# A decoder layer with a retrieval of experts: a new flow of gathers, copies moved beside the last heads, and work of the first stages dealt out anew

## The chip, the core and the metric

The kernel runs on one core of a Trainium2 chip. The metric is the device time of one execution in microseconds (us), lower is better. TensorE multiplies matrices into PSUM, VectorE and ScalarE (ACT) work on vectors, GpSimd (POOL) also issues the gathers, SyncE (SP) issues most other transfers.

## The reference

One layer of a hybrid decoder on 512 tokens of width 2048, in 32-bit floats: adaLN (a shift, a scale and a gate per feature from the vector c), a joint projection into differential attention and an mLSTM, an output projection, and a retrieval of experts (PEER). Cut to what the change touches:

```python
cs = silu(c)
mod = (cs @ w_ada[l] + b_ada[l]).reshape(B, 6, D)
sh_m, sc_m, gt_m, sh_f, sc_f, gt_f = [mod[:, i] for i in range(6)]
h = modulate(rms_norm(x, g_mix[l]), sh_m, sc_m)          # h * (1 + scale) + shift
p = einsum('bsd,dp->bsp', h, w_in[l])
...
h2 = modulate(rms_norm(x, g_ffn[l]), sh_f, sc_f)
x = x + gt_f[:, None, :] * peer(h2, w_pq[l], sub_keys[l], peer_u[l], peer_v[l])

def peer(h, ...):             # 8 heads, 16 of 128 x 128 experts for each token and head
    s = einsum('thcd,hcnd->thcn', q, sub_keys)
    s_top, i_top = top_k(s, 16)                           # for each half of the query
    sc, pos = top_k(all 256 sums, 16); idx = the 16 experts; g = softmax(sc)
    a = gelu(einsum('td,thkd->thk', h, peer_u[idx]))
    return einsum('thk,thkd->td', g * a, peer_v[idx])
```

## The kernel before, in words

An fp32 product is three matmuls (mm3, L112 to L114) of operands split into a high and a low part: ACT casts the high part (wh, hh, Wh), VectorE subtracts it from the raw value for the low part (wl, hl, Wl). Weights come in blocks of 128 x 1024 (wr), loaded by SP, split by ACT and VectorE (L121, L123, L132).

**First stages (to 186 us).** A loop over the 16 kt (blocks of 128 features) multiplies x by seven column blocks of the input projection, whose sums stay in PSUM (acc0), and makes the adaLN columns meanwhile: `ada_load` fetches a row block of w_ada in two halves of 128 x 1024, `ada_half` (L221) multiplies each by cs and sums it on VectorE, and `mod_one` adds the two sums and the bias (L245) and, for a scale, 1 and the gain (L250). After the loop `h_full` makes the hi and lo parts of the shifted rows for each kt (hh on ACT at L418, hl on VectorE at L421, with a column's two halves before and after it), and VectorE multiplies the seven PSUM blocks by rb, the tokens' reciprocal norms (L498).

**Heads, lead halves and hot loop (966 to 1528 us).** PEER computes gelu(U h2) for all 16384 experts and the 368 tokens TD, scatters the gates into a dense table gd, and multiplies by V. The other tokens, 128 in one block and 16 more, gather their experts' rows from U and V in DRAM instead (`gather_load`, a gather of 128 rows of 8 KB issued by GpSimd, and `gather_use`, one 2048-wide VectorE instruction: a dot product with h2row for a row of U at L1438, a sum into h2row for a row of V at L1447). While VectorE picks the top k of the last heads, TensorE computes slices of U h2 ahead (`lead_half`, 24 matmuls each, stored in leadd). Behind the heads come the rows that the gathers need: sums h3 and h3e of hh and hl (L1295, L1339), turned by TensorE into h2row and h2e, and three key transposes ijg (If, Jf and Gf with their low parts, L1319 to L1328). The hot loop then builds one-hot tables on VectorE and gd on TensorE, with a lead half in each of its iterations, and 23 gathers; the lead halves that are left follow.

**Main loop (1528 to 3310 us).** 256 steps: a step multiplies 4 x 256 rows of V by the weighted activations W (24 matmuls `ps_mm`), adds the two PSUM results into yT on VectorE (L1676), and, once the lead slices are used up, computes half a slice of U h2 (24 matmuls `ps_ax`) AHEAD steps ahead. `w_slice` multiplies a finished slice by its gates and splits it (L1504 to L1507); `v_split` makes the hi and lo parts of V for the next step (L1534, L1535). A gather is bound to the first matmul of a step and used in the next:

```python
gdue += SLOW if st_ < n_slow else rate
while gdue >= 1.0 and gk < NGA:
    gather_load(gk, first)
```

Each gathered row passes through one of two buffers (gbp). When all are used, `out_gathered` finishes the 128 gathered tokens in parts; part 6 is three 2048-wide GpSimd instructions (L1579 to L1581). SP, ACT and GpSimd each work off their instructions, transfers among them, in the written order.

Of the kernel before, what the change touches and what calls it, by code (L numbers as in the profile page):

```python
# [85 lines left out]
def hymba_layer(ctx: ExitStack, tc: tile.TileContext, I, out: bass.AP):  # L86
# [155 lines left out]
    def mod_one(sec, kt, gcol=None):  # L242
        c0 = SEC[sec] * KT + kt
        m = modc[:, c0 : c0 + 1]
# [42 lines left out]
    adap = sA.enter_context(tc.tile_pool(name="adap", bufs=5, side="right"))  # L287
# [209 lines left out]
    for b in (4, 5, 0, 1, 2, 3, 6):  # L497
        nc.vector.tensor_tensor(mlqk[:, b, :], acc0[b], rb, op=ALU.mult)  # L498
# [719 lines left out]
    def lead_half():  # L1218
# [605 lines left out]
```

## Time and profile before

| | before |
|---|---|
| median of 3 runs | 3370.25 us (3361.97 to 3375.71) |
| profiled execution, its time | 3366.22 us |
| its span in the trace | 3364.1 us |
| TensorE busy | 3236.9 us (96%) |
| VectorE busy | 2800.0 us (83%) |
| ScalarE busy | 1184.3 us (35%) |
| GpSimd busy | 597.1 us (18%) |
| mean granted TensorE clock | 0.981 |
| HBM | 263 GB/s over the span |

The span runs from the first instruction to the last on the core; the execution's own time is 2.1 us longer. A busy share is a mean over stages, and the stages of this kernel differ. Times in rows are microseconds from the span's start. A granted clock of 1.0 is 2.4 GHz, 0.5 is 1.2 GHz, and values between are means over a stretch.

### The profile page before, as it was taken

Reading aid. Unit: us, or ns where it says so; the run is one execution under the profiler, and the core shown is the slowest. Engines: PE = TensorE matmul, PEld = TensorE weight load, DVE = VectorE, ACT = ScalarE, POOL = GpSimd, SP = SyncE. Lnnn points to the kernel's source line nnn. Section 1 sums busy time; section 2 is a strip of 40 time slices with the busy share of each in tenths; the row PEclk is TensorE's granted clock in tenths of the full one; section 3 lists DMA queues with packets and bytes.
Section 4 is the critical chain, followed back from the end, with each engine's and each line's share of the span. In section 5 each row is a group of like instructions: output and inputs, shape, how many; then the busy total and the mean of one; then the engine's idle time right before and its main releaser. Section 6 shows DMA issues by size and latency. Waiting matters only on the chain.

```text
span 3364.1 us, 48080 instructions
## 1 busy us (share of the span) xinstructions
PE 3236.9 (96%) x18323; PEld 2986.1 (89%) x18323; DVE 2800.0 (83%) x4661; ACT 1184.3 (35%) x1745; POOL 597.1 (18%) x410
## 2 busy tenths in 40 slices
PE   8899999999899989999999999999999999999996
PEld 6677876788778889989999999999999999999995
DVE  8968699987669989977887888888888888888867
ACT  3223343333232347763332323232232232332323
POOL 0000133100024411011111222221122221122104
PEclk9899999999999989999999999999999999999997
DMA  8866666769722339897777888888988889888944
GB/s 333 286 229 206 209 222 226 247 231 317 255 89 89 105 129 302 294 310 274 275 270 273 321 323 319 316 324 323 328 319 308 319 312 338 317 325 314 330 159 137
DMA packets 261191, 891.45 MB, mean 265 GB/s; under 512 B 24145, under 2 KB 91361, under 8 KB 223969
## 3 DMA queue, kind: packets, MB, share of 16 engines
q1 hardware_dynamic: 219490, 586.39, 49.8%
q0 software_dynamic: 41472, 302.01, 25.3%
q8 instruction: 144, 2.36, 0.3%
q14 instruction: 85, 0.70, 0.1%
HBM read 843.75 MB, written 40.35 MB: 263 GB/s over the span
## 4 chain that ended last, share of the span: by engine, by line
PE 58%; DVE 26%; DMA 10%; issue 4%; ACT 2%; POOL 0%; SPq 0%; DVEq 0%; ACTq 0%; POOLq 0%
PE ps_mm L112 12%; PE ps_mm L114 12%; PE ps_mm L113 12%; PE ps_ax L112 6%; PE ps_ax L113 6%; PE ps_ax L114 6%; DMA gb<-in_vN_dram,gx 3%; DMA gb<-in_uN_dram,gx 3%; DVE gb L1438 2%; DVE wl L123 2%; DVE wl L132 2%; DVE ohi L1380 1%; DVE ada L221 1%; DVE wr L221 1%; DVE hl L1535 1%
## 5 line engine op out<-in xcount | busy, mean ns | idle before, releaser
L112 PE MATMUL ps_ax<-hh,wh 128*128 128x368 f32 (+1 forms) x2112 | 708.0, 335 | 19.1 <-ACT wh L121 10.6
L114 PE MATMUL ps_ax<-hh,wl 128*128 128x368 f32 (+1 forms) x2112 | 705.1, 334 | 14.1 <-DVE wl L123 7.9
L113 PE MATMUL ps_ax<-hl,wh 128*128 128x368 f32 (+1 forms) x2112 | 702.8, 333 | 0.0
L114 PE MATMUL ps_mm<-Wh,hl 128*128 128x368 f32 x2048 | 680.8, 332 | 11.3 <-DVE hl L1535 10.2
L112 PE MATMUL ps_mm<-Wh,hh 128*128 128x368 f32 x2048 | 680.1, 332 | 11.7 <-ACT Wh L1506 7.9
L113 PE MATMUL ps_mm<-Wl,hh 128*128 128x368 f32 x2048 | 677.1, 331 | 0.7
L121 ACT CAST wh<-wr 128x1024 fp32r<-128x1024 f32 (+1 forms) x418 | 436.8, 1046 | 391.5 <-PE ps_ax L113 133.4
L123 DVE TENSOR_TENSOR wl<-wr,wh 128x1024 fp32r<-128x1024 f32 (+1 forms) x317 | 396.9, 1253 | 145.3 <-ACT wh L121 144.2
L114 PEld LDWEIGHTS ps_ax<-hh,wl 128*128 128x128 f32 x2112 | 399.6, 189 | 24.8 <-DVE wl L123 9.0
L112 PEld LDWEIGHTS ps_ax<-hh,wh 128*128 128x128 f32 x2112 | 399.9, 189 | 23.8 <-ACT wh L121 11.8
L113 PEld LDWEIGHTS ps_ax<-hl,wh 128*128 128x128 f32 x2112 | 399.8, 189 | 3.0
L114 PEld LDWEIGHTS ps_mm<-Wh,hl 128*128 128x128 f32 x2048 | 386.5, 189 | 16.7 <-DVE hl L1535 14.6
L112 PEld LDWEIGHTS ps_mm<-Wh,hh 128*128 128x128 f32 x2048 | 386.9, 189 | 13.7 <-ACT Wh L1506 9.3
L113 PEld LDWEIGHTS ps_mm<-Wl,hh 128*128 128x128 f32 x2048 | 386.5, 189 | 2.7 <-DVE Wl L1507 2.6
L1447 DVE SCALAR_TENSOR_TENSOR h2row<-gb,ga,h2row 128x2048 f32<-128x2048 f32 x127 | 298.2, 2348 | 80.2 <-DMA gb<-in_vN_dram,gx 78.0
L112 PE MATMUL ps_mm<-hh,wh 128*128 128x512 f32 x832 | 336.1, 404 | 9.5 <-ACT hh L410 5.8
L1535 DVE TENSOR_TENSOR hl<-vr,hh 128x1024 fp32r<-128x1024 f32 x254 | 316.8, 1247 | 25.0 <-ACT hh L1534 23.8
L113 PE MATMUL ps_mm<-hl,wh 128*128 128x512 f32 x832 | 331.5, 398 | 2.8 <-DVE hl L452 2.8
L1438 DVE SCALAR_TENSOR_TENSOR gb<-gb,h2row 128x2048 f32<-128x2048 f32 x128 | 292.3, 2287 | 49.5 <-DMA gb<-in_uN_dram,gx 49.4
L1423 POOL DMA_INDIRECT gb<-in_uN_dram,gx x128 | 171.6, 1340 | 905.0 <-PE ps_mm L112 259.4
L114 PE MATMUL ps_mm<-hh,wl 128*128 128x512 f32 x832 | 330.6, 397 | 0.2 <-DVE wl L123 0.2
L1534 ACT CAST hh<-vr 128x1024 fp32r<-128x1024 f32 x256 | 268.2, 1048 | 117.8 <-PE ps_mm L113 97.0
(342 smaller groups left out, 4346.8 us busy)
## 6 DMA issues: line engine op xcount, KB each, us to landing
wr<-in_uT_dram SPq DMA_DIRECT2D x256, 512.0 KB
vr<-in_vB_dram SPq DMA_DIRECT2D x256, 512.0 KB
wr<-in_adaT_dram SPq DMA_DIRECT2D x192, 512.0 KB
ada<-in_adaT_dram SPq DMA_DIRECT2D x66, 512.0 KB
wr<-in_winN_dram SPq DMA_DIRECT2D x48, 512.0 KB
gd<-Gs SPq DMA_DIRECT2D x12, 2048.0 KB
g<-gd SPq DMA_DIRECT2D x32, 768.0 KB
wr<-in_winT_dram SPq DMA_DIRECT2D x32, 512.0 KB
```

Source lines behind the costliest of these rows:

```text
L112: ins = nc.tensor.matmul(ps, wh, xh, start=first, stop=False)
L113: nc.tensor.matmul(ps, wh, xl, start=False, stop=False)
L114: nc.tensor.matmul(ps, wl, xh, start=False, stop=last)
L121: nc.scalar.copy(hi, raw)
L123: (lo_eng or nc.vector).tensor_tensor(lo, raw, hi.bitcast(F32), op=ALU.subtract)
L132: eng.tensor_tensor(lo, raw, hi.bitcast(F32), op=ALU.subtract)
L221: nc.vector.scalar_tensor_tensor(w, w, 1.0, cs[:, q * (D // 2) : (q + 1) * (D // 2)], op0=ALU.mult, op1=ALU.mult, accum_out=modr[:, q, col ...
L1423: ins = nc.gpsimd.indirect_dma_start(out=buf.rearrange("p k c -> p (k c)"), out_offset=None, in_=I["vN"] if n else I["uN"], in_offset=bass ...
L1438: nc.vector.scalar_tensor_tensor(buf, buf, 1.0, row, op0=ALU.mult, op1=ALU.mult, accum_out=gate[:, c : c + 1])
L1447: nc.vector.scalar_tensor_tensor(row, buf, gate[:, c : c + 1], row, op0=ALU.mult, op1=ALU.add)
L1534: nc.scalar.copy(hi, raw)
L1535: (nc.gpsimd if few and i % 2 else nc.vector).tensor_tensor(lo, raw, hi.bitcast(F32), op=ALU.subtract)
```

## The change

1. An adaLN column of the first stages is one buffer of 128 x 2048 (two of them instead of five halves), still loaded in two transfers, and summed by one VectorE instruction; `mod_one` is one instruction, since the bias gets its 1 once at the start. ACT copies the seven PSUM blocks out, and VectorE multiplies them by rb later, in the convolution's first stage.
2. The sums of hh and hl for the gathered tokens (`h2_sum`) and their turns (`h2_turn`) stand in the loop of the last heads. Before the hot loop only the first key transpose is left; the other two and gxe are in the hot loop. One lead half fewer stands before the hot loop, one more behind it.
3. The lead slices are stored from ACT's queue instead of SP's.
4. In the lead loop and the main loop two gathers are always in flight: `gather_next` uses one and issues the one after the next, with no tie to a matmul. In a step with two, the first use stands ahead of `w_slice`, and the other between the two additions into yT. SLOW is 0.4 instead of 0.35.
5. AHEAD is 10 instead of 9.

```diff
+    def ada_full(w, col):
+        nc.vector.scalar_tensor_tensor(
+            w, w, 1.0, cs, op0=ALU.mult, op1=ALU.mult, accum_out=modr[:, 0, col : col + 1],
+        )
...
-        nc.vector.scalar_tensor_tensor(
-            m, modr[:, 0, c0 : c0 + 1], modr[:, 1, c0 : c0 + 1], cols[:, C_BADA + c0 : C_BADA + c0 + 1],
-            op0=ALU.add, op1=ALU.add,
-        )
...
+            nc.vector.scalar_tensor_tensor(m, w, b, cols[:, gcol + kt : gcol + kt + 1], op0=ALU.add, op1=ALU.mult)
...
-    adap = sA.enter_context(tc.tile_pool(name="adap", bufs=5, side="right"))
+    adap = sA.enter_context(tc.tile_pool(name="adap", bufs=2, side="right"))
...
     for b in (4, 5, 0, 1, 2, 3, 6):
-        nc.vector.tensor_tensor(mlqk[:, b, :], acc0[b], rb, op=ALU.mult)
+        nc.scalar.copy(mlqk[:, b, :], acc0[b])
...
+            nc.vector.tensor_tensor(x, x, rb, op=ALU.mult)
             nc.scalar.activation(x, x, AF.Identity, bias=bet[:, 0, b : b + 1])
...
-            nc.sync.dma_start(leadd[n // 2], lead["la"])
+            nc.scalar.dma_start(leadd[n // 2], lead["la"])
...
+    extra = [lambda: h2_sum(0), lambda: None, lambda: h2_turn(0, h2row), lambda: h2_sum(1), lambda: None, lambda: h2_turn(1, h2e)]
     lead_half()
     start_head(*due.pop(0))
     back.run(3.9)
     s_pump(1)
     while back.gens:
         lead_half()
+        if extra:
+            extra.pop(0)()
...
     for n in range(0, NG, 2):
+        if n % (P // NHOT) == 8 and n // (P // NHOT) < ND - 1:
+            ijg_make(pk, n // (P // NHOT) + 1)
+        if n == 4:
+            nc.vector.tensor_copy(gxe, gef[:, 0, :])
...
-    AHEAD = 9
+    AHEAD = 10
...
-    SLOW = 0.35
-    gdue, gnew = 0.0, []
+    SLOW = 0.4
+    gu, gdue = gk, 0.0
+
+    def gather_next():
+        nonlocal gu
+        gather_use(gu)
+        gu += 1
+        if gu + 1 < NGA:
+            gather_load(gu + 1)
...
+        gdue += SLOW if st_ < n_slow else rate
+        ng = min(int(gdue), NGA - gu)
+        gdue -= ng
+        if ng > 1:
+            gather_next()
+
         if h % 2 == 0 and h // 2 - 1 >= JB and st_ < NH:
             w_slice(h // 2 - 1)
         elif st_ == NH and h % 2 == 0:
             w_slice(h // 2 - 1)
-        for k in gold:
-            gather_use(k)
...
                 nc.vector.tensor_tensor(y[:, 0:TD], y[:, 0:TD], pss[q][:, 0:TD], op=ALU.add)
+            if q == 0 and ng:
+                gather_next()
...
-        gold = gnew
-        gnew = []
-        if gk < NGA:
-            gdue += SLOW if st_ < n_slow else rate
-            while gdue >= 1.0 and gk < NGA:
-                gather_load(gk, first)
```

The order of instructions at three places, in which names are tiles and Lxxx are each kernel's own lines.

VectorE at the end of the kt loop, before: wl and wgc, the last x_norm, the column's halves (ada), the shift of kt 0 (modc), hl of kt 0, and the multiplies of the PSUM blocks.

```order
L123 TENSOR_TENSOR wl<-wr,wh 128x1024
L471 TENSOR_TENSOR wgc<-wg,wgc 128x16x8
L429 SCALAR_TENSOR_TENSOR xT<-xT,modc,ps_ax 128x512 x2
L221 SCALAR_TENSOR_TENSOR ada,modr<-ada,cs 128x1024 x2
L245 SCALAR_TENSOR_TENSOR modc<-modr,cols 128x1
L221 SCALAR_TENSOR_TENSOR ada,modr<-ada,cs 128x1024
L421 SCALAR_TENSOR_TENSOR hl<-xT,modc,hh 128x512
L221 SCALAR_TENSOR_TENSOR ada,modr<-ada,cs 128x1024
L498 TENSOR_TENSOR mlqk<-ps_ax,rb 128x512 x2
L498 TENSOR_TENSOR mlqk<-ps_mm,rb 128x512 x4
L498 TENSOR_TENSOR mlqk<-ps_ax,rb 128x512
```

After the change, the same place on VectorE:

```order
L431 SCALAR_TENSOR_TENSOR xT<-xT,modc,ps_ax 128x512 x2
L227 SCALAR_TENSOR_TENSOR ada,modr<-ada,cs 128x2048
L249 TENSOR_TENSOR modc<-modr,cols 128x1
L227 SCALAR_TENSOR_TENSOR ada,modr<-ada,cs 128x2048
L425 SCALAR_TENSOR_TENSOR hl<-xT,modc,hh 128x512
L249 TENSOR_TENSOR modc<-modr,cols 128x1
L227 SCALAR_TENSOR_TENSOR ada,modr<-ada,cs 128x2048
L425 SCALAR_TENSOR_TENSOR hl<-xT,modc,hh 128x512
L249 TENSOR_TENSOR modc<-modr,cols 128x1
```

And on ACT, from hh of kt 0 to that of kt 1 and the next ones:

```order
L422 ACTIVATE hh<-xT,modc 128x512
L500 COPY mlqk<-ps_ax 128x512 x2
L500 COPY mlqk<-ps_mm 128x512 x4
L500 COPY mlqk<-ps_ax 128x512
L422 ACTIVATE hh<-xT,modc 128x512 x3
```

The seven multiplies have left VectorE, and seven copies stand on ACT between hh of kt 0 and hh of kt 1.

VectorE ahead of the hot loop, before: from gx (the rows to gather) to the first one-hot tables (ohj, ohe); h and h3e are the sums, rem belongs to the key transposes, wl to lead halves.

```order
L1292 SCALAR_TENSOR_TENSOR gx<-If,Jf 128x128
L1293 COPY gw_7647<-Gf 128x128
L1295 TENSOR_TENSOR h_10026<-hh,hl 128x2048
L1301 SCALAR_TENSOR_TENSOR geq<-If,Jf 128x128
L1304 COPY geq<-Gf 128x128
L1312 TENSOR_REDUCE sel<-ident 128x16
L123 TENSOR_TENSOR wl<-wr,wh 128x1024
L1324 TENSOR_TENSOR rem<-ps_mm,ijg_10076 128x128
L1326 TENSOR_TENSOR rem<-rem,ijg_10076 128x128
L1324 TENSOR_TENSOR rem<-ps_mm,ijg_10087 128x128
```

...and after these, two rem more, two wl, h3e, gxe and ib. After the change, from gx to the one-hot tables:

```order
L1331 SCALAR_TENSOR_TENSOR gx<-If,Jf 128x128
L1332 COPY gw_7573<-Gf 128x128
L1334 SCALAR_TENSOR_TENSOR geq<-If,Jf 128x128
L1337 COPY geq<-Gf 128x128
L123 TENSOR_TENSOR wl<-wr,wh 128x1024
L1352 TENSOR_TENSOR rem<-ps_mm,ijg_10048 128x128
L1354 TENSOR_TENSOR rem<-rem,ijg_10048 128x128
L123 TENSOR_TENSOR wl<-wr,wh 128x1024
L1369 CAST ib<-iota 128x512
L1380 TENSOR_TENSOR ohj<-ib,ijg_10048 128x512 x2
L1389 TENSOR_TENSOR ohe<-ib,ijg_10048 128x512
```

The sums, gxe and two pairs of rem have left this place.

VectorE in two steps of the main loop, before: L1438 is a use of a gather, L1676 the additions into yT.

```order
L1438 SCALAR_TENSOR_TENSOR gb,ga_7646<-gb,h2row 128x2048
L1676 TENSOR_TENSOR yT<-yT,ps_mm 128x368 x2
L123 TENSOR_TENSOR wl<-wr,wh 128x1024
L1535 TENSOR_TENSOR hl<-vr,hh 128x8x128
L1438 SCALAR_TENSOR_TENSOR gb,ga_7646<-gb,h2row 128x2048
L1676 TENSOR_TENSOR yT<-yT,ps_mm 128x368 x2
L123 TENSOR_TENSOR wl<-wr,wh 128x1024
L1535 TENSOR_TENSOR hl<-vr,hh 128x8x128
```

After the change, where L1448 is the use and L1702 the additions:

```order
L1702 TENSOR_TENSOR yT<-yT,ps_mm 128x368
L1448 SCALAR_TENSOR_TENSOR gb,ga_7572<-gb,h2row 128x2048
L1702 TENSOR_TENSOR yT<-yT,ps_mm 128x368
L123 TENSOR_TENSOR wl<-wr,wh 128x1024
L1549 TENSOR_TENSOR hl<-vr,hh 128x8x128
L1448 SCALAR_TENSOR_TENSOR gb,ga_7572<-gb,h2row 128x2048
L1702 TENSOR_TENSOR yT<-yT,ps_mm 128x368
L1448 SCALAR_TENSOR_TENSOR gb,ga_7572<-gb,h2row 128x2048
L1702 TENSOR_TENSOR yT<-yT,ps_mm 128x368
L123 TENSOR_TENSOR wl<-wr,wh 128x1024
L1549 TENSOR_TENSOR hl<-vr,hh 128x8x128
```

A use now stands between the two additions, with wl and hl of the step behind it.

## Rows read from the trace of the kernel before

**Rows 1.** The page, chain that ended last: share of the span by engine and line.

```profile
PE ps_mm L112 12%; PE ps_mm L114 12%; PE ps_mm L113 12%; PE ps_ax L112 6%; PE ps_ax L113 6%; PE ps_ax L114 6%; DMA gb<-in_vN_dram,gx 3%; DMA gb<-in_uN_dram,gx 3%; DVE gb L1438 2%; DVE wl L123 2%; DVE wl L132 2%; DVE ohi L1380 1%; DVE ada L221 1%; DVE wr L221 1%; DVE hl L1535 1%
```

**Rows 2.** Windows: stretch, its length, busy time by engine (count), TensorE clock, DMA share, GB/s.

```profile
16.00:113.00 97.00, 85.68 (x355) 66.99 (x355) 94.27 (x177) 35.09 (x51) 0.00 (x0) 0.97 0.86 317
1118.00:1208.00 90.00, 73.48 (x407) 71.06 (x406) 87.91 (x395) 30.84 (x37) 33.55 (x14) 0.88 0.31 99
1208.00:1234.00 26.00, 21.44 (x115) 21.11 (x115) 12.80 (x21) 10.69 (x22) 0.45 (x1) 0.76 0.28 90
1234.00:1495.00 261.00, 256.87 (x2220) 244.43 (x2219) 252.68 (x367) 199.12 (x253) 31.32 (x25) 1.00 0.87 288
1800.00:3225.00 1425.00, 1418.40 (x8462) 1414.31 (x8461) 1197.64 (x1305) 426.77 (x530) 296.05 (x238) 1.00 0.87 318
3293.00:3310.00 17.00, 8.29 (x29) 7.21 (x28) 15.01 (x11) 1.97 (x3) 10.48 (x3) 0.60 0.59 197
```

**Rows 3.** Timeline of TensorE, first matmuls of V in two steps: start, duration.

```profile
3289.02 0.33 PE L112 MATMUL ps_mm<-Wh,hh 128*128 128x368 f32 x1
...
3293.02 0.33 PE L112 MATMUL ps_mm<-Wh,hh 128*128 128x368 f32 x1
```

**Rows 4.** Groups of instructions, 1800 to 3225 us: count, busy, mean ns, idle before.

```profile
L114 PE MATMUL ps_mm<-Wh,hl 128*128 128x368 f32 x1408 | 465.9, 331 | 6.4 <-DVE hl L1535 6.2
...
L1447 DVE SCALAR_TENSOR_TENSOR h2row<-gb,ga,h2row 128x2048 f32<-128x2048 f32 x127 | 298.2, 2348 | 80.2 <-DMA gb<-in_vN_dram,gx 78.0 <-issue 1.9
...
L1438 DVE SCALAR_TENSOR_TENSOR gb<-gb,h2row 128x2048 f32<-128x2048 f32 x80 | 182.7, 2288 | 49.5 <-DMA gb<-in_uN_dram,gx 49.4
```

**Rows 5.** Timeline of VectorE, two halves of a column and what follows: start, duration.

```profile
59.98 1.22 DVE L221 SCALAR_TENSOR_TENSOR ada<-ada,cs 128x1024 f32<-128x1024 f32 x1
...
62.39 0.22 DVE L245 SCALAR_TENSOR_TENSOR modc<-modr,cols 128x1 f32<-128x1 f32 x1
...
62.75 1.09 DVE L132 TENSOR_TENSOR wl<-wr,wh 128x896 fp32r<-128x896 f32 x1
```

**Rows 6.** Timeline of VectorE around the multiplies of L498.

```profile
109.28 0.75 DVE L421 SCALAR_TENSOR_TENSOR hl<-xT,modc,hh 128x512 fp32r<-128x512 f32 x1
...
111.08 1.28 DVE L498 TENSOR_TENSOR mlqk<-ps_ax,rb 128x512 f32<-128x512 f32 x2
...
115.28 0.21 DVE L245 SCALAR_TENSOR_TENSOR modc<-modr,cols 128x1 f32<-128x1 f32 x1
```

**Rows 7.** Chain that ended last: start, time for which a transfer held it, which.

```profile
197.77 5.57 DMA wr<-in_adaT_dram
...
1494.10 16.80 DMA gd<-Gs
...
2506.70 10.71 DMA gb<-in_vN_dram,gx
...
3067.30 5.45 DMA gb<-in_vN_dram,gx
```

**Rows 8.** Timeline of VectorE between the heads and the hot loop.

```profile
1209.21 2.29 DVE L1295 TENSOR_TENSOR h<-hh,hl 128x2048 f32<-128x2048 f32 x1
...
1217.78 0.29 DVE L1324 TENSOR_TENSOR rem<-ps_mm,ijg 128x128 f32<-128x128 f32 x1 [0.74 <-ACT ijg L1322]
...
1219.47 0.29 DVE L1324 TENSOR_TENSOR rem<-ps_mm,ijg 128x128 f32<-128x128 f32 x1 [0.74 <-ACT ijg L1322]
...
1226.88 2.28 DVE L1339 TENSOR_TENSOR h3e<-hh,hl 128x2048 f32<-128x2048 f32 x1
```

**Rows 9.** Timeline of step 248: GpSimd, VectorE and TensorE.

```profile
3289.94 4.60 POOL L1579 TENSOR_TENSOR x<-x,rb 128x2048 f32<-128x2048 f32 x1 [77.67 <-ACT rb L1578]
...
3290.84 9.34 DVE L1535 TENSOR_TENSOR hl<-vr,hh 128x1024 fp32r<-128x1024 f32 x2 [5.08 <-ACT hh L1534]
...
3306.07 1.22 DVE L1535 TENSOR_TENSOR hl<-vr,hh 128x1024 fp32r<-128x1024 f32 x1
...
3304.74 0.67 PE L112 MATMUL ps_mm<-Wh,hh 128*128 128x368 f32 x1 [6.55 <-ACT Wh L1506]
```

More of the change, by code (lines that the diff above doesn't have):

```diff
@@ L1279, in hymba_layer, with h2_sum, h2_turn @@
     pkl = sL.enter_context(tc.tile_pool(name="pkl", bufs=2, side="right", reuse_waits="tile"))
+    NE = PH * TK // NR
+    s3 = slice(TY, T)
+    h2row = gp.tile([P, KT, P], F32, name="h2row")
+    h2e = gep.tile([P, KT, P], F32, tag="h2e", name="h2e")
+    gef = gep.tile([P, 2, NE], F32, name="gef")
+    gxe = gep.tile([P, NE], I32, name="gxe")
+    gae = gep.tile([P, NE], F32, name="gae")
+    sel = gep.tile([P, TE], F32, name="sel")
+    y3 = h2row
+    hs = {}
+    def h2_sum(n):
+        hs[n] = gbp.tile([P, KT, P], F32, tag="gb", name="hs")
+        hhf, hlf = hh.bitcast(F32), hl.bitcast(F32)
+        if n == 0:
+            nc.vector.tensor_tensor(hs[n], hhf[:, :, s3], hlf[:, :, s3], op=ALU.add)
+        else:
+            nc.vector.tensor_tensor(
+                hs[n].rearrange("p k (r t) -> p k r t", t=TE),
+                hhf[:, :, TD:TY].unsqueeze(2).to_broadcast([P, KT, NR, TE]),
+                hlf[:, :, TD:TY].unsqueeze(2).to_broadcast([P, KT, NR, TE]), op=ALU.add,
+            )
+            nc.vector.reduce_sum(sel, ident.rearrange("p (r t) -> p t r", t=TE), axis=AX.X)
+    def h2_turn(n, dst):
+        for q in range(4):
+            pw = bank("mm")
+            for r in range(4):
+                nc.tensor.transpose(pw[:, r * P : (r + 1) * P], hs[n][:, 4 * q + r, :], ident)
+            nc.scalar.copy(dst[:, 4 * q : 4 * q + 4, :], pw.rearrange("p (k c) -> p k c", k=4))
+    extra = [lambda: h2_sum(0), lambda: None, lambda: h2_turn(0, h2row), lambda: h2_sum(1), lambda: None, lambda: h2_turn(1, h2e)]
     lead_half()
@@ L1426, in gather_load @@
         )
-        tc.add_manual_dep(
-            ins.ins, after.ins.name,
-            mybir.DependencyInfo(mybir.DependencyClass.Sync, mybir.DependencyReason.SCHED_ONLY), reason="pace",
-        )
+        if after is not None:
+            tc.add_manual_dep(
+                ins.ins, after.ins.name,
+                mybir.DependencyInfo(mybir.DependencyClass.Sync, mybir.DependencyReason.SCHED_ONLY), reason="pace",
+            )
         gbuf[k] = buf
@@ L1666, in hymba_layer @@
             w_slice(h // 2 - 1)
-        for k in gold:
-            gather_use(k)
         for q in range(QV):
@@ L1694, in hymba_layer @@
                 s_pump(1)
-        gold = gnew
-        gnew = []
-        if gk < NGA:
-            gdue += SLOW if st_ < n_slow else rate
-            while gdue >= 1.0 and gk < NGA:
-                gather_load(gk, first)
-                gnew.append(gk)
-                gk += 1
-                gdue -= 1.0
-        elif not gold and not last and x3 is None:
+        if gu == NGA and not last and x3 is None:
             out_gathered(0)
```

78 lines of the change are left out of this document (25 added, 53 removed).

## The prediction

> **What bounds the kernel now.** I read the chain that ended last first [rows 1]: matmuls on TensorE lead it, VectorE and the gathers come next. Then the stretches [rows 2]. In 1800 to 3225 us, 42% of the span, TensorE is busy 1418.40 of 1425 us at full clock. One step there is 24 + 24 matmuls, and 24 start within 4.00 us [rows 3], so a step needs 8.00 us; 176 steps were done (1408 of V's third matmuls [rows 4], eight in a step), 1408 us, which leaves at most 17 us to win. The reader is to see in [rows 4] that VectorE waits 80.2 + 49.5 us for gathers there, while TensorE waits 6.4 us for hl. So most of VectorE's waiting costs nothing.
>
> The other stretches differ [rows 2]. From 16 to 113 us VectorE is busy 94.27 of 97 us, from 1118 to 1208 us 87.91 of 90: VectorE sets the pace. From 1208 to 1234 us nobody does: TensorE 21.44 of 26 us at a granted clock of 0.76, VectorE 12.80. In the hot loop, 1234 to 1495 us, both are nearly full (256.87 and 252.68 of 261). So VectorE's work has its full price in the first two and in the hot loop, and hardly any in the main loop.
>
> **The change, part by part.** The sum is made against the profiled execution, 3366.22 us; the median of the three runs, 3370.25, lies 4.03 us higher, and the result is moved up by that.
>
> A, first stages. The two halves of an adaLN column take from 59.98 to 62.39 = 2.41 us, the two column instructions from 62.39 to 62.75 = 0.36 us [rows 5]. A 2048-wide instruction of that kind (L1438) takes 2.29 us [rows 4], one column instruction about 0.17. That saves 0.12 + 0.19 = 0.3 us per kt, 16 times: -5. The seven multiplies out of PSUM (L498) hold VectorE from 111.08 to 115.28 = 4.2 us [rows 6]. ACT makes these copies now; it is busy 35.09 of 97 us before [rows 2], so it has the room. But hl of kt 0, at 109.28, then stands behind a whole column of 2.29 us instead of a half (+1.1), and ACT makes hh of kt 1 only after its seven copies. Of the 4.2 us I count 4 if loads are in time; the 1.1 us, and what the copies hold up hh, I leave to the range, since the kt 1 column itself stands 4 us earlier. Against both: two whole buffers replace five halves. A half's load was waited for 5.57 us on the chain, at 197.77 [rows 7]; a buffer's turn is then 5.57 + 2.29 = 7.9 us, and with two of them a column comes every 3.9 us. In the kt loop (16 kt in 97 us, one column per 6 us) that is hidden. Where only one hl stands between columns (2.29 + 0.75 + 0.17 = 3.2 us) 0.7 us per column are lost; at six such columns +4. A = -5 - 4 + 4 = **-5**, from -9 (loads land in time) to 0 (twice as many columns late). The seven multiplies come back in the convolution, 0.6 us each, beside projections in which TensorE leads: 0, at most +4 where that cover is gone.
>
> C, around the hot loop. From the 26 us between 1208 and 1234 go h3 and h3e, 2.29 and 2.28 us [rows 8], their turns on TensorE, two of three key transposes with their chain (one per 1.69 us, 1217.78 to 1219.47), and one of the three lead halves there. What is left is two halves of 4.00 us, at the granted clock 0.76 10.5 us, a transpose and four small instructions, 1 us: 11.5 us, so -14.5. The sums now stand beside the last heads, where VectorE is 98% busy: 2.29 + 2.28 us and a short reduction, +5 in full; their turns are TensorE's work in a stretch in which it waits, 0. The two other key transposes and gxe stand in the hot loop, which is full: 2 x 1.69 + 0.2 = +3.6, at least 0 if they find gaps. One more lead half stands behind the hot loop: +4. That is -14.5 + 5 + 3.6 + 4 = -1.9. At full clock the two halves would take 2.5 us less, and with TensorE waiting less before them I count 1 of it: C = **-3**, from -8 (key transposes hidden, clock up) to +4.
>
> D, queues. The store of a lead slice goes from SP's queue to ACT's. The stall that it stood beside is a 16.80 us transfer of gd, at 1494.10 [rows 7], for which g waits; it stays. 0, within 3 either way: behind a store on ACT stand the casts wh and hh, which VectorE and then TensorE wait for, at perhaps 0.4 us each.
>
> F, the flow of gathers. Before, a gather was issued at the pace of a step's first matmul and used in the next step, ahead of the y adds; now two are always in flight, each issued when the use two before it is done. A gather's landing held the chain 5.45 to 10.71 us, at 3067.30 and 2506.70 [rows 7]. Of four uses in three steps one is tight: its load goes out at the end of a use that stands behind the first y add of one step, and it is used at the same place of the next step, 8.1 - 2.35 (L1447) = 5.75 us later [rows 4]. The others have over 8 us. At a landing of 7 us VectorE waits 1.3 us, at 10.7 us 5 us; behind it stand the second y add, wl and hl, whose next use is about 4 us off. So the waiting moves from ahead of the y adds, which free TensorE's PSUM banks, to a place with slack. 6.4 us of the 17 are visible as TensorE's wait for hl [rows 4]; where the rest lies no view says. I take half of 17, near the visible part: **-8**, from -12 to 0. Earlier steps have VectorE to spare, 0.
>
> G, the tail. Three GpSimd instructions of 4.5 us start at 3289.94 [rows 9]; the two hl next to them take 9.34 us instead of 1.22 each, slice 127's Wh comes only behind them, and TensorE waits 6.55 us for it at 3304.74. From 3293 to 3310 us TensorE is busy 8.29 us, at a clock of 0.60 [rows 2], for step 248, which needs 4.0, and half a us of the next: 12.5 us are lost. With AHEAD at 10 slice 127 is prepared when two steps of V alone are still to come, 8 us of cover instead of 4, and the GpSimd instructions start two steps earlier. They take 13.6 us and can still meet an hl, so I leave 3.5 us: **-9**, from -5 to -12.5.
>
> The Trainium skill, SBUF — State Buffer, section "SBUF: two separate sides", says that VectorE and GpSimd share one pair of ports as a lock, held for a whole instruction, which hits VectorE's instructions with two SBUF inputs when the GpSimd one reads SBUF. The trace agrees: 9.34 / 2 = 4.67 us for each hl, the length of one GpSimd instruction [rows 9]. By that rule any hl that meets one of the three in their new place costs 3.4 us more, which is about what G leaves.
>
> Sum: -5 - 3 + 0 - 8 - 9 = -25, 3366.2 - 25 = 3341; with the 4 us to the median **3345 us**.
>
> **The rivals.**
> Nothing from the gathers. For it: TensorE waited only 6.4 us there. Against: 17 us lie over 8.00 us per step. F = 0 gives 3353. Chance 0.11.
>
> Early gains given back. Two buffers bind VectorE at 3.9 us per column through the whole of 113 to 186 us too, A = +1; the 5 us beside the heads and 3.6 in the hot loop come in full, and the clock falls again, C = +3: 3345 + 12 = 3357. For it: these stretches are VectorE's. Against: fewer instructions there in all. 0.12.
>
> Slower: late gathers ahead of wl and hl. A use stands between the y adds now, and the step's wl and hl behind it. If tight landings take 10 us as a rule (10.71 was seen), VectorE's wait passes its 4 us of slack, and TensorE loses 0.5 to 1 us in each of 176 / 3 = 58 groups, +29 to +58 where -8 stood: 3345 + 8 + 43 = 3396. It decides from a landing of 5.75 + 4 = 9.75 us on. For it: loads go out closer together. Against: bytes and gathers are the same in number, and VectorE is busy 1197.64 of 1425 us. 0.08.
>
> The Trainium skill, DMA: Bandwidth & Descriptors, section "Anatomy of one DMA — SWDGE (gpsimd) path", gives a transfer from GpSimd's queue 2.0 us plus its bytes over 436e3 per us; for a gather of 128 rows of 8 KB that is an estimate of 4.4 us, by which no gather would be waited for and the time would be 3345 or less. The trace differs, 5.45 to 10.71 us beside the transfers of the weights [rows 7], and the measurement decides.
>
> More gain. The whole 17 us of the main loop, G at -12.5, A at -9: 3345 - 9 - 3.5 - 4 = 3328. 0.09.
>
> **How the numbers follow.** The forecast has 0.60, with a range of its own of 3333 to 3357 (A, C, F and G are not all at one end together). A measurement of this kernel can hardly tell less than 0.5%, 16.9 us, from no change: faster is under 3353.4, slower over 3387.1. Faster: 0.60 x 0.92 + 0.09 + half of 0.11 = 0.69. Same: 0.60 x 0.08 + the other half of 0.11 + 0.12 = 0.23. Slower: 0.08. For 8 in 10 the range reaches from 3322, below the best case, to 3366, over both cases without gain; the slow case and single ends beyond these hold under 0.2.
>
> **What would show it.** A: the column is one instruction of 2.3 us and no multiply stands at 111; wrong if VectorE's idle time before 186 us names the ada loads for more than 5 us. C: the hot loop begins about 10 us earlier, less A's gain, and lasts 3 to 4 us longer. F: a mean step of 8.05 us instead of 8.10 from 1800 us on, VectorE's waits for gathers mostly behind the first y add; wrong if TensorE waits there over 10 us for hl or wl. G: the step that took 16.5 us takes 5 to 8, and TensorE waits nowhere near 6 us for Wh. The forecast as a whole fails if tight landings are over 10 us as a rule, or if GpSimd's three instructions meet the hl of both last V-only steps.

## The result and the profile after

The changed kernel takes 3329.62 us (median of 6 runs, 3319.92 to 3340.36), the kernel before, measured beside it, 3369.95 us: a ratio of 0.9885, 95% interval 0.9859 to 0.991, some 40 us or 1.2% less. Forecast were 3345 us and a range of 3322 to 3366. The profiled execution took 3333.74 us, its span is 3331.9 us, 32.2 less than before; the analysis below is of this pair of executions. Three executions ran slower, at a mean granted clock of 0.56 to 0.88 instead of 0.98 (one of part 2 alone, two of the kernel before); they count in the medians of the next section, but not in its ratios, from which its gains in us are worked out.

The page of the changed kernel, first the engines, then the chain that ended last:

```profile
PE 3225.4 (97%) x18323; PEld 2979.4 (89%) x18323; DVE 2786.5 (84%) x4579; ACT 1190.6 (36%) x1752; POOL 521.2 (16%) x411
...
PE 70%; DVE 20%; DMA 5%; ACT 3%; issue 2%; POOL 0%; SPq 0%; ACTq 0%; DVEq 0%; POOLq 0%
PE ps_mm L112 15%; PE ps_mm L113 15%; PE ps_mm L114 15%; PE ps_ax L112 8%; PE ps_ax L114 8%; PE ps_ax L113 8%; DVE gb L1448 2%; DVE wl L123 1%; DVE ada L227 1%; DVE wl L132 1%; ACT wh L121 1%; DMA wr<-in_uT_dram 1%; DVE ohi L1390 1%; DMA wr<-in_winT_dram 1%; DVE wr L221 1%
```

TensorE's share of the chain rises from 58% to 70%, and the gathers, 3% and 3% in [rows 1], are no longer among its first entries. The same stretches as in [rows 2], with their ends moved as the stages moved (columns as there):

```profile
1118.00:1208.00 90.00, 73.78 (x434) 71.15 (x432) 88.04 (x393) 35.84 (x45) 35.14 (x14) 0.92 0.30 99
1208.00:1227.00 19.00, 18.77 (x98) 18.60 (x99) 10.05 (x23) 6.25 (x10) 1.11 (x1) 0.84 0.53 170
1227.00:1482.00 255.00, 248.80 (x2169) 235.56 (x2169) 247.92 (x363) 196.56 (x255) 27.53 (x24) 1.00 0.87 289
1800.00:3210.00 1410.00, 1410.00 (x8417) 1410.00 (x8416) 1184.52 (x1287) 425.65 (x527) 225.18 (x232) 1.00 0.88 317
3268.00:3285.00 17.00, 17.00 (x104) 17.00 (x103) 12.13 (x18) 6.46 (x9) 4.27 (x3) 1.00 0.90 321
```

Between heads and hot loop 19 us are left of 26, and TensorE works through them (18.77 us). The hot loop leaves both engines 6 to 7 of 255 us idle, as full as before. From 1800 to 3210 us TensorE has no idle time by the profile, and the stretch behind step 247, of which it was busy 8.29 of 17 us, is full. The groups of the main loop, 1790 to 3213 us, as in [rows 4]:

```profile
L114 PE MATMUL ps_mm<-Wh,hl 128*128 128x368 f32 x1408 | 465.2, 330 | 0.0
...
L1457 DVE SCALAR_TENSOR_TENSOR h2row<-gb,ga,h2row 128x2048 f32<-128x2048 f32 x127 | 298.1, 2347 | 6.1 <-DMA gb<-in_vN_dram,gx 5.4
...
L1448 DVE SCALAR_TENSOR_TENSOR gb<-gb,h2row 128x2048 f32<-128x2048 f32 x75 | 171.5, 2286 | 4.3 <-DMA gb<-in_uN_dram,gx 4.1
```

VectorE's waits for gathers fell from 80.2 + 49.5 to 6.1 + 4.3 us, TensorE's wait for hl from 6.4 us to nothing.

The first matmul of V in each step and the first and last of each stage, in the timeline of TensorE, give an account of the 32.2 us. The single parts were run by themselves (next section); what each did at the same place stands beside it.

| stretch | before | after | difference | the part alone | forecast |
|---|---|---|---|---|---|
| start to the end of the stage at 185 us | 184.8 | 181.3 | -3.5 | part 1: -3.4 | A -5 |
| from there to the first lead half | 933.6 | 936.4 | +2.8 | part 1: +0.4 | 0 |
| lead halves beside the heads, to the hot loop | 122.9 | 109.3 | -13.7 | part 2: -14.0 | C -9.5 |
| hot loop | 251.3 | 254.9 | +3.5 | part 2: +2.9 | C +3.6 |
| hot loop's end to step 62 | 291.2 | 293.9 | +2.7 | part 2: +2.1 | C +4, less 1 |
| steps 62 and 63 | 18.8 | 17.3 | -1.5, with one computed half (4.0) more: -5.5 | part 5: -5.8 | none |
| steps 64 to 247 | 1490.4 | 1479.3 | -11.2, with one half less: -7.1 | part 4: -4.9; part 5, with one half less: -4.9 | F -8 |
| step 248 | 16.5 | 4.0 | -12.5 | part 4: -12.3; part 5: -12.5 | G -9 |
| the rest | 54.6 | 55.7 | +1.1 | | |

One trace of each kernel stands in this table; how far its rows carry, all fourteen traces of this document show. With part 1 the first stage ends at 179.1 to 181.7 us (nine traces), without it at 183.3 to 186.0 (five). From the first lead half to the hot loop it is 106.4 to 109.9 us with part 2, 120.3 to 123.1 without. Step 248 takes 4.0 to 4.2 us with part 4 or 5, 16.1 to 16.8 without. But the first lead half begins anywhere from 1115.3 to 1122.3 us in eight traces whose code is the same up to there, so that the second row says little by itself.

### The profile page after: what moved, and what is told of

Read it like the earlier page. It is cut to its first block, busy times and chain, and to the rows that moved or that the text cites. A ratio compares the mean times of both kernels' runs of the same rounds, so it can differ in the third digit from the quotient of the medians.

```text
span 3331.9 us, 47966 instructions
## 1 busy us (share of the span) xinstructions
PE 3225.4 (97%) x18323; PEld 2979.4 (89%) x18323; DVE 2786.5 (84%) x4579; ACT 1190.6 (36%) x1752; POOL 521.2 (16%) x411
## 4 chain that ended last, share of the span: by engine, by line
PE 70%; DVE 20%; DMA 5%; ACT 3%; issue 2%; POOL 0%; SPq 0%; ACTq 0%; DVEq 0%; POOLq 0%
PE ps_mm L112 15%; PE ps_mm L113 15%; PE ps_mm L114 15%; PE ps_ax L112 8%; PE ps_ax L114 8%; PE ps_ax L113 8%; DVE gb L1448 2%; DVE wl L123 1%; DVE ada L227 1%; DVE wl L132 1%; ACT wh L121 1%; DMA wr<-in_uT_dram 1%; DVE ohi L1390 1%; DMA wr<-in_winT_dram 1%; DVE wr L221 1%
## 5 line engine op out<-in xcount | busy, mean ns | idle before, releaser
L121 ACT CAST wh<-wr 128x1024 fp32r<-128x1024 f32 (+1 forms) x418 | 437.0, 1046 | 448.0 <-PE ps_ax L113 199.2
L1448 DVE SCALAR_TENSOR_TENSOR gb<-gb,h2row 128x2048 f32<-128x2048 f32 x128 | 292.6, 2286 | 4.3 <-DMA gb<-in_uN_dram,gx 4.1
L1432 POOL DMA_INDIRECT gb<-in_uN_dram,gx x128 | 129.0, 1008 | 899.4 <-DVE gb L1448 593.4
```

Source lines behind the costliest of these rows:

```text
L121: nc.scalar.copy(hi, raw)
L1432: ins = nc.gpsimd.indirect_dma_start(out=buf.rearrange("p k c -> p (k c)"), out_offset=None, in_=I["vN"] if n else I["uN"], in_offset=bass ...
L1448: nc.vector.scalar_tensor_tensor(buf, buf, 1.0, row, op0=ALU.mult, op1=ALU.mult, accum_out=gate[:, c : c + 1])
```

## The experiments

Each time is a median beside runs of the kernel before on the same chip, each ratio has its 95% interval; what a part did in a stretch is read from one profiled execution each.

**One part alone on the kernel before.** Part 1 (columns, copies on ACT) without the others:

```diff
-    adap = sA.enter_context(tc.tile_pool(name="adap", bufs=5, side="right"))
+    adap = sA.enter_context(tc.tile_pool(name="adap", bufs=2, side="right"))
...
-        nc.vector.tensor_tensor(mlqk[:, b, :], acc0[b], rb, op=ALU.mult)
+        nc.scalar.copy(mlqk[:, b, :], acc0[b])
```

> The kernel before with part 1 of the change alone (columns in one instruction, copies on ACT, multiplies in the convolution). Theory 1: the end of the stage at 113 to 186 us comes 3 to 4 us earlier, with about 5 us of VectorE's waiting for column loads in it, and at the first lead half only 0 to 1 us is left, because the multiplies lengthen VectorE's convolution and the stall of TensorE near 290 us grows from 3 to about 7 us. Rival, as forecast: 5 us remain to the end.

Measured: 3365.7 us against 3367.63, ratio 0.9992 (0.9982 to 1.0003). In this trace the stage ends 3.4 us earlier, 3.1 us of it are there at the first lead half and 3.5 at step 64, behind which the old flow of gathers took 3.5 us longer in this execution. That alone would refute theory 1, but all traces together bear it out: the nine with part 1 end the stage 4.1 us earlier on average than the five without it, and begin the first lead half 1.0 us earlier. From the end of the stage to 420 us TensorE is idle for 9.2 to 11.2 us in the nine and 7.2 to 7.9 in the five. The seven multiplies stand there now (243.7 to 290.8 us in the changed kernel), and one stall of TensorE right behind them takes 6.0 us here instead of 2.8 (another of 2.0 goes). So some 2.5 us are given back in the convolution, and the rival's 5 us to the end are not seen. The other loss against the forecast is in the loads, whose groups in the changed kernel, 16 to 182 us on VectorE, are:

```profile
L227 DVE SCALAR_TENSOR_TENSOR ada<-ada,cs 128x2048 f32<-128x2048 f32 x32 | 73.2, 2288 | 5.1 <-DMA ada<-in_adaT_dram 5.0
...
L123 DVE TENSOR_TENSOR wl<-wr,wh 128x1024 fp32r<-128x1024 f32 (+1 forms) x11 | 13.2, 1210 | 8.0 <-ACT wh L121 7.9
```

and in the kernel before, 16 to 186 us:

```profile
L221 DVE SCALAR_TENSOR_TENSOR ada<-ada,cs 128x1024 f32<-128x1024 f32 x64 | 76.7, 1218 | 0.0
...
L123 DVE TENSOR_TENSOR wl<-wr,wh 128x1024 fp32r<-128x1024 f32 (+1 forms) x11 | 13.2, 1209 | 5.1 <-ACT wh L121 5.0
```

32 columns wait 5.1 us in all, 5.0 of them for their loads (7.0 in part 1 alone), where the halves waited 0.0, near the forecast's +4; the wl that follow wait 8.0 us (6.1 in part 1 alone), 5.1 before. The prediction had named more than 5 us of such waiting as its sign that A is wrong: the changed kernel stands at that limit, part 1 alone is over it.

Part 2 (sums and turns beside the heads, two key transposes in the hot loop):

```diff
+    extra = [lambda: h2_sum(0), lambda: None, lambda: h2_turn(0, h2row), lambda: h2_sum(1), lambda: None, lambda: h2_turn(1, h2e)]
...
+        if extra:
+            extra.pop(0)()
```

> The kernel before with part 2 alone (sums, turns and key transposes moved). Theory 1: the hot loop begins about 14 us earlier, takes 3 to 4 us more, and with the extra lead half 6 to 8 us are left at the first step of the main loop or soon after it. Rival, as forecast: the 5 us of sums lengthen the heads in full, the hot loop begins 9 to 10 us earlier, and 3 us are left.

Measured: 3357.38 us, ratio 0.9972 (0.9954 to 0.9989), 9 us. The hot loop begins 14.7 us earlier, takes 2.9 us more, and 9.7 us are left at step 62. Theory 1 holds, with 9.0 us gained from the first lead half to step 62 in place of its 6 to 8. From the first lead half to gx, with which the heads are done on VectorE, it is 92.6 us instead of 90.5 (92.2 in the changed kernel; 89.5 to 93.2 in the nine traces with part 2, 90.2 to 91.5 in the five without): of the 5 us of sums 1 to 2 us lengthen the heads. The traces show where the rest went. Part of VectorE's busy time there is time in which GpSimd holds its instructions up; the kernel before, GpSimd and VectorE:

```profile
1141.15 2.37 POOL L123 TENSOR_TENSOR wl<-wr,wh 128x1024 fp32r<-128x1024 f32 x1 [0.33 <-ACT wh L121]
...
1141.22 2.46 DVE L1164 CAST ab<-ab 128x256 bf16<-128x256 f32 x1
```

and the same cast in the changed kernel, as a group from 1118 to 1208 us:

```profile
L1167 DVE CAST ab<-ab 128x256 bf16<-128x256 f32 x3 | 0.9, 284 | 0.0
```

Nine instructions of VectorE, from the first lead half to gx, are stretched like this in the kernel before, each beside a wl of GpSimd and ending within 0.3 us behind its end: together they last 17.1 us longer than the shortest of their kind (16.8 to 18.1 us in the traces without part 2). In the changed kernel there are seven, with 14.1 us (13.6 to 15.2 in the traces with part 2). So some 3 of the 5 us came out of that.

Part 4 (gathers, AHEAD still 9):

```diff
-        for k in gold:
-            gather_use(k)
...
+            if q == 0 and ng:
+                gather_next()
```

> The kernel before with part 4 alone (two gathers in flight, uses between the additions), AHEAD still 9. Theory 1: the gather flow takes 10 us of TensorE's waits out of steps 64 to 247, and some 5 us out of the two steps in which the first computed half begins; GpSimd's three instructions start two steps earlier, so that step 248 loses at most 4 us even without AHEAD 10: 20 to 25 us in all. Rival: step 248 needs AHEAD 10, and keeps 8 to 12 us of its loss here: 10 to 15 us in all.

Measured: 3348.6 us, ratio 0.9937 (0.9917 to 0.9956), 21 us. Step 248 takes 4.2 us, with AHEAD 9. Timeline of GpSimd, the three instructions of the gathered tokens' end:

```profile
3260.18 5.48 POOL L1593 TENSOR_TENSOR x<-x,rb 128x2048 f32<-128x2048 f32 x1 [69.84 <-ACT rb L1592]
3265.73 4.48 POOL L1594 TENSOR_TENSOR x<-x,modc 128x2048 f32<-128x2048 f32 x1
3270.29 4.48 POOL L1595 TENSOR_TENSOR x<-x,modc 128x2048 f32<-128x2048 f32 x1
```

The last use comes earlier (in step 236 instead of 239), so they start in step 244 instead of step 247 [rows 9], beside steps of 8 us. Theory 1 is right in the total and in step 248. It is right on TensorE's waits, too: of the steps 64 to 236 thirteen took 8.1 to 10.1 us in the kernel before, which lost 9.9 us, and here none takes over 8.07. But 4 us of that are given back, since all of these steps ran at 8.05 us here and nearly half of them at 8.00 before ("Two rhythms", below), so that the table has -4.9. Steps 62 and 63 gain 1 us only, not the 5 that theory 1 gave this part.

Part 5 (AHEAD 10, and the fifth slice loaded in time for it):

```diff
-    AHEAD = 9
+    AHEAD = 10
...
+    lead_load(JB)
```

> The kernel before with part 5 alone (AHEAD 10, and the fifth slice's load before the main loop, which it needs). Theory 1: GpSimd's three instructions still meet hl at step 248, so step 248 keeps 4 to 8 of its 12.5 us, and the two steps at 1784 to 1802 us still lose 6 to 7 us: 4 to 8 us gained. Rival: AHEAD by itself takes away the whole 12.5 us, and the loss at 1784 to 1802 us too, since the computed halves begin at an even step: 12 to 18 us.

Measured: 3349.45 us, ratio 0.995 (0.9932 to 0.9967), 17 us. It takes step 248's loss too, but not all of its cause; timeline of GpSimd, VectorE and TensorE:

```profile
3276.05 4.81 POOL L1579 TENSOR_TENSOR x<-x,rb 128x2048 f32<-128x2048 f32 x1 [73.80 <-ACT rb L1578]
...
3278.24 0.33 PE L114 MATMUL ps_mm<-Wh,hl 128*128 128x368 f32 x1
...
3285.49 4.47 POOL L1581 TENSOR_TENSOR x<-x,modc 128x2048 f32<-128x2048 f32 x1
...
3290.89 0.44 PE L112 MATMUL ps_mm<-Wh,hh 128*128 128x368 f32 x1 [1.53 <-DVE yT L1677]
```

The three instructions still begin in the last steps, each hl beside them takes 3.7 us, and 5.7 us are lost in steps 250 and 251, whose additions into yT come late. And it takes away 5.8 us in steps 62 and 63, which theory 1 had put down to the gathers and the rival to AHEAD: the rival was right. In steps 64 to 247 it gains 4.9 us as well, with the old flow of gathers: eight long steps lose 4.2 us, where the four traces with the old flow and AHEAD 9 lose 9.9 to 16.3 us in 13 to 17 of them.

**The two covers of step 248 against each other.** The changed kernel with AHEAD 9:

```diff
-    AHEAD = 10
+    AHEAD = 9
```

> The changed kernel with AHEAD 9 again (and without the fifth slice's early load). Theory 1, after part 4 alone had taken step 248's loss away: the new gather flow already starts GpSimd's three instructions at step 244, so step 248 loses under 2 us; the two steps in which the first computed half begins lose some 5 us again: 5 to 8 us slower than the changed kernel. Rival, as the terms of the forecast have it: AHEAD is what covers step 248, which loses 9 us here: 12 us or more slower.

Measured: 3337.14 us against 3371.95, ratio 0.99 (0.9871 to 0.9928); the trace is 6.1 us longer than the changed kernel's. Step 248 takes 4.2 us and step 246 loses 0.9, so together 1.1; the two steps in which the computed halves begin lose 5.5 us more. (The stretches before them were 4.3 us longer by chance, and a faster rhythm, below, gave 5 back.) Theory 1 holds: beside the new flow AHEAD 10 is worth 1 us at the end, and 5 to 6 where the computed halves begin.

**The loss where the computed halves begin.** The kernel before, with the first computed slice's loads a step earlier:

```diff
-    V0, V1 = 2, n_slow - 2
+    V0, V1 = 2, n_slow - 3
```

> The kernel before, with the loads of the first computed slice issued one step earlier (V1 one less), nothing else. Theory 1: the 6 to 7 us lost at 1784 to 1802 us are these loads landing 3 us too late for ACT, whose cast wh stands ahead of hh of the next step: with one step (4 us) more, under 2 us are lost there, and the kernel is 4 to 6 us faster. Rival: the loss comes with the gather or the parity of the step and stays.

The timeline of ACT and TensorE there, of the kernel before:

```profile
1788.19 1.04 ACT L121 CAST wh<-wr 128x1024 fp32r<-128x1024 f32 x1 [4.97 <-DMA wr<-in_uT_dram]
...
1791.48 0.68 PE L112 MATMUL ps_mm<-Wh,hh 128*128 128x368 f32 x1 [3.52 <-ACT hh L1534]
```

and with the earlier loads (PEld is TensorE's load of weights):

```profile
1783.35 1.05 ACT L121 CAST wh<-wr 128x1024 fp32r<-128x1024 f32 x1 [3.94 <-DMA wr<-in_uT_dram]
...
1786.65 0.19 PEld L112 LDWEIGHTS ps_mm<-Wh,hh 128*128 128x128 f32 x1 [0.43 <-ACT hh L1534]
```

ACT works in order: its cast wh (L121) waits 4.97 us for the load, hh of the next V (L1534) stands behind it, and TensorE waits 3.52 us for hh. With the loads a step earlier the wait is 0.43 us, the two steps lose 1.8 us instead of 6.8, and the time is 3361.02 us, ratio 0.9976 (0.9961 to 0.9991). Theory 1 holds. (The trace as a whole is 4.8 us longer than that of the kernel before: it reached the first lead half 3.8 us later, and the old flow took 6.7 us more in steps 64 to 247.) With AHEAD 10 the load is issued 9.2 us ahead of the step instead of 7.6 (11.15 less the wait of 3.52), and lands sooner; the trace of part 5 alone:

```profile
1776.84 1.05 ACT L121 CAST wh<-wr 128x1024 fp32r<-128x1024 f32 x1 [0.85 <-DMA wr<-in_uT_dram]
...
1781.58 0.43 PE L114 MATMUL ps_mm<-Wh,hl 128*128 128x368 f32 x1 [0.77 <-DVE hl L1535]
```

The same edit on the changed kernel:

> The changed kernel with the loads of the first computed slice one step earlier (V1 one less). Theory 1: what is left of the loss where the computed halves begin, 1.3 us at step 62, goes: 1 to 1.5 us faster in the trace, too little for the median to tell. Rival: an earlier load takes the buffer of a V block and a stall of over 2 us appears in the steps before.

Measured: 3341.37 us against 3365.54, ratio 0.9903 (0.9864 to 0.9941). The rival holds: the stall is gone at step 62 and 4.2 us are lost in steps 60 and 61 instead.

**Place or time in flight.** The changed kernel, with all uses of a step ahead of both additions:

```diff
-            if q == 0 and ng:
-                gather_next()
...
+        for k in range(ng):
+            gather_next()
```

> The changed kernel with a step's uses of gathers ahead of both additions again, as before the change, but still two gathers in flight. Theory 1, the step of the forecast: it is the place behind the first addition that has slack; here VectorE's waits hold TensorE's banks again, TensorE waits 5 us or more for hl in steps 64 to 240, and the kernel is 5 to 10 us slower than the changed one. Rival: it is the longer time in flight; VectorE's waits for gathers stay under 40 us (146 before the change, 11 behind it), TensorE waits under 1 us for hl, and the time is that of the changed kernel within 4 us.

Measured: 3333.48 us, ratio 0.9883 (0.9844 to 0.9922), the trace 1.1 us shorter than the changed kernel's. Its groups from 1800 to 3210 us:

```profile
L114 PE MATMUL ps_mm<-Wh,hl 128*128 128x368 f32 x1400 | 463.2, 331 | 0.3 <-DVE hl L1549 0.2
...
L1457 DVE SCALAR_TENSOR_TENSOR h2row<-gb,ga,h2row 128x2048 f32<-128x2048 f32 x127 | 298.2, 2348 | 63.9 <-DMA gb<-in_vN_dram,gx 63.3
...
L1448 DVE SCALAR_TENSOR_TENSOR gb<-gb,h2row 128x2048 f32<-128x2048 f32 x74 | 168.7, 2287 | 31.3 <-DMA gb<-in_uN_dram,gx 31.3
```

VectorE waits 64 + 31 us, with the 16 tokens' gathers 111, more than the 40 of the rival, but TensorE waits 0.3 us for hl and the time is that of the changed kernel. So the place spares VectorE's waits and buys no time, beside AHEAD 10. Part 5 alone has AHEAD 10 and the old place as well, and in the main loop differs from this kernel in the issue of the gathers alone (two in flight, no tie to a matmul, SLOW): its long steps lose 4.2 us, the two here 0.8. So the issue buys time; how much of the 9.9 us of the kernel before is its own and how much AHEAD 10's, one trace of each does not settle, and the old place with AHEAD 9 was not run.

**The store's queue.** The changed kernel with the lead slices stored by SP:

```diff
-            nc.scalar.dma_start(leadd[n // 2], lead["la"])
+            nc.sync.dma_start(leadd[n // 2], lead["la"])
```

> The changed kernel with the lead slices stored from SP's queue again. Theory 1, as forecast for part 3: no difference within 3 us, the time between the end of the hot loop and the first step of the main loop is 43 us as in the changed kernel, give or take 3. Rival: the store on SP delays the loads behind it, and 3 to 6 us are lost there.

Measured: 3335.07 us, ratio 0.9895 (0.9862 to 0.9929). From the hot loop's end to step 0 it is 44.8 us instead of 43.3; the first six steps then take 2.6 us more (steps 2 and 4 5.07 and 6.21 us, against 4.00 and 4.08). From the hot loop's end to step 6 that makes 72.3 us, where the seven other traces of the changed kernel and its variants take 66.6 to 69.1. That speaks for the rival, in one trace; by the medians' ratios (0.9895 and 0.9885) the intervals overlap. What part 3 is worth, some 4 us or less, stays open.

**Two rhythms.** In the full steps of the changed kernel TensorE never waits, and yet a step takes 8.05 us instead of 8.00. The kernel again, with matmuls added that shift the stream and change no result:

> The changed kernel with one more matmul ahead of V's in the steps 70, 105, 140, 175 and 210, of 16, 48, 96, 160 and 256 columns, which overwrites what the next one clears. Theory 1: the 24 matmuls of V run in one of two rhythms, 4.00 or 4.05 us, set by where the stream of matmuls stands, and a small shift can flip it: after some of the five steps the following ones take 8.00 us instead of 8.05, up to 1.8 us less per 35 steps; a flip back may follow. Rival: the 0.05 us comes from the new order of VectorE's or GpSimd's instructions, and all steps stay at 8.05.

```diff
+            if q == 0 and st_ in (70, 105, 140, 175, 210):
+                n_ = {70: 16, 105: 48, 140: 96, 175: 160, 210: 256}[st_]
+                nc.tensor.matmul(ps[:, 0:n_], vh[:, 0], Wt[b][0][:, 0, 0:n_], start=True, stop=True)
```

Measured: 3329.38 us, ratio 0.9886 (0.9863 to 0.9908). This execution came out of step 62 at 8.00 us a step; the shift of 96 columns at step 140 turned it to 8.05, that of 160 at step 175 back to 8.00, the three others changed nothing. So a shift of the stream can turn the rhythm, and theory 1 holds.

> The changed kernel itself, a second profiled execution. Theory 1: the rhythm of the full steps (8.00 or 8.05 us) is set by where the last stall left the stream, so another execution may show 8.00 and then gains up to 9 us; the stretch from 186 to 1118 us differs by up to 3 us with nothing changed in it. Rival: the rhythm belongs to the kernel: 8.05 again in all full steps.

Measured: the second execution of the changed kernel (3335.66 us) runs 8.05 us in all full steps too, as the rival has it. But the run with the five matmuls, whose code is that of the changed kernel up to step 70, came out of step 62 at 8.00 us: the rhythm does not belong to the kernel, and on this theory 1 holds. The second execution reached the first lead half 2.3 us later than the first, with nothing changed; from the end of the first stage to there it took 4.1 us more, over the 3 of theory 1.

```diff
+            if q == 0 and st_ == 66:
+                nc.tensor.matmul(ps[:, 0:160], vh[:, 0], Wt[b][0][:, 0, 0:160], start=True, stop=True)
```

> The changed kernel with one more matmul of 160 columns ahead of V's in step 66, which overwrites what the next one clears. Theory 1: the full steps begin in the slow rhythm (8.05 us, as in two executions of the changed kernel), and this shift puts them into the fast one: 8.00 us from step 67 on, 170 x 0.053 = 9 us less in the trace, and some 5 to 9 us less in the median if most executions begin in the slow rhythm. Rival: a shift of 160 columns doesn't flip it from this starting place, or it flips back at once: 8.05 and the time of the changed kernel.

Timeline of TensorE, the first matmul of V in two steps that follow each other, of the changed kernel:

```profile
2098.99 0.33 PE L112 MATMUL ps_mm<-Wh,hh 128*128 128x368 f32 x1
...
2107.04 0.33 PE L112 MATMUL ps_mm<-Wh,hh 128*128 128x368 f32 x1
```

and of the kernel with the one added matmul:

```profile
2100.08 0.33 PE L112 MATMUL ps_mm<-Wh,hh 128*128 128x368 f32 x1
...
2108.08 0.33 PE L112 MATMUL ps_mm<-Wh,hh 128*128 128x368 f32 x1
```

8.05 against 8.00 us, from step 67 on as expected, 9 us in all. Of these the steps 238 to 240, into which other work falls, took 3 us back, and the stretches before step 64 2.9 us by chance. Median 3325.86 us, ratio 0.988 (0.986 to 0.9899): the lowest of all kernels here, but not told apart from the changed kernel's 0.9885.

## Why the prediction was right

The direction and the range held. The sum was too small, -25 forecast against -32 in the profiled pair and -39 by the ratio: two terms were too small and one missing, all on the same side. One term, F, came out at its size by luck, and two reasons were wrong.

**A, -5: the mechanism right, the sizes not.** The stage ended 3.5 us earlier in the profiled pair. Windows from 16 us to its end, before and after (columns as in [rows 2]):

```profile
16.00:184.77 168.77, 151.57 (x613) 115.91 (x613) 157.62 (x284) 55.02 (x75) 0.00 (x0) 0.95 0.83 297
16.00:181.28 165.28, 150.57 (x613) 115.47 (x613) 146.88 (x198) 58.40 (x82) 0.00 (x0) 0.95 0.83 303
```

VectorE's work fell by 10.7 us, more than the 9 of the forecast: a column cost what was worked out (2.29 us and one column instruction), but the sum counted 16 columns and the stage has 32. Its idle time grew by 7.2 us, more than the 4, mostly 5 us for the columns' loads and 3 more for wh. The multiplies in the convolution were set at 0 and cost some 2.5 us there, so that only about 1 us of A is left at the first lead half.

**C, -3: right in its parts, one of them mis-sized.** The removal, -14.5, measured -15.3 from gx to the hot loop (32.4 to 17.1 us), and the key transposes cost the hot loop 2.9 to 3.5 us of the 3.6. The step that failed was "+5 in full" beside the heads: VectorE is 98% busy there before and after (87.91 and 88.04 of 90 us), yet the heads grew by 1 to 2 us, since 17 of its busy us were time in which its instructions were held up beside GpSimd, and only 14 are now. With that the part gives 7.5 us in the changed kernel's trace and 9 us alone, in its trace and by its ratio.

**F, -8: the size right by luck, the reason wrong.** Steps 64 to 247 gained 7.1 us, and the full steps wait for nothing. The long steps' 9.9 us are gone, but 4.3 us were lost to the rhythm: of the 174 steps from 64 to 237, 81 ran at 8.00 us before and none after. The prediction took the whole 17 us over 8.00 us a step for what the gathers might win at most; half of it happens to lie near what the two leave. And "to a place with slack" was not what did it: the uses moved back ahead of the additions gave the same time. The tight landing of 5.75 us hardly mattered (11 us of VectorE's waits in 176 steps). What did it is the new issue of the gathers and, as far as one trace tells, also AHEAD 10, each worth 4.9 us alone. The slower rival, landings of 10 us as a rule, did not occur: with the uses moved, a gather took 7.0 to 7.8 us from issue to landing in the median.

**G, -9: measured -12.5, by another cause than named.** I gave it to AHEAD 10 and its 8 us of cover. The new flow of gathers alone gives -12.3, since it starts GpSimd's three instructions in step 244; with it, AHEAD 9 loses 1 us there. That they can still meet an hl was right, and the steps of 8 us carry it; in the changed kernel, GpSimd and VectorE:

```profile
3253.36 4.79 POOL L1605 TENSOR_TENSOR x<-x,rb 128x2048 f32<-128x2048 f32 x1 [74.04 <-ACT rb L1604]
...
3254.50 4.75 DVE L1549 TENSOR_TENSOR hl<-vr,hh 128x1024 fp32r<-128x1024 f32 x1
```

The hl begins 1.14 us behind GpSimd's instruction, takes 4.75 us in place of 1.22 [rows 9], and ends 1.10 us behind its end; TensorE does not wait. The Trainium skill, SBUF — State Buffer, section "SBUF: two separate sides", has the one that starts first hold the shared ports for its whole instruction and the other blocked, where VectorE's has two SBUF inputs and GpSimd's reads SBUF. This trace agrees: the hl lasts as long as the rest of GpSimd's instruction, 3.65 us, and 1.10 us more.

**Missing: -5.5 where the computed halves begin.** The prediction took the two steps at 1784 us as unchanged. Their loss was one load landing behind ACT's turn, and part 5 moved it out (-5.8 alone); the run with only the load moved, on the kernel before, shows the cause: 5.0 of the 6.8 us went.

By their ratios the four parts alone add up to 0.08 + 0.28 + 0.63 + 0.5 = 1.5%, 50 us, and the whole change gives 1.15%, 39 us. Step 248's 12.5 us stand in part 4 and in part 5, which is about the difference.

**Not settled:** what part 3 is worth, how the new issue and AHEAD 10 share the 9.9 us of the long steps, and what decides the rhythm.

## What to carry to other kernels

When two parts of a change remove the same stall, each alone shows its whole price: run each alone and one taken out of the whole, before a gain is put down to either. A wait of the engine that is not the bound is worth removing only where it reaches the one that is: 100 us less of VectorE's waiting for gathers made no difference in time between two kernels here, while one load that was late for ACT's next instruction cost 5 us. Work put beside an engine that reads 98% busy does not always lengthen it: look first how much of that is instructions held up by another engine. And a forecast of some us for a stage wants the spread of that stage over several executions beside it.

## What the runs showed of the hardware

A steady stream of 24 + 24 matmuls, with no wait in the records and at a granted clock of 1.00, ran in one of two rhythms, 8.00 or 8.05 us a step, and kept it for a hundred steps and more. The 0.05 us lie in V's 24 matmuls (4.00 or 4.05 us). In the kernel before the rhythm turned at stalls; in two other traces it also turned once with no wait in the records. A single added matmul of 96 or 160 columns turned it, those of 16, 48 and 256 columns did not (160 was tried twice, the others once). Over 176 steps that is 9 us, a quarter of what the whole change gained. What in the stream's place decides it no run shows.

VectorE's instructions that begin beside one of GpSimd can last until that one ends: beside the heads a cast of 0.28 us took 2.46, and nine such instructions lasted 17 us longer than their shortest, and all of that reads as VectorE's busy time.

Executions of the same code differ by up to 7 us at the first lead half (1115.3 to 1122.3 us in eight traces), where nothing was changed; so a term under 7 us that adds up to that place cannot be read from one trace of this kernel.
